# The first feed-forward's gates kept in the tile of the convolution's diagonals, its sums of rows a chunk later, and gate casts behind the PSUM copies

## The chip, the cores and the metric

The kernel runs on one core of one Trainium2 chip. Its engines are TensorE (PE, whose weight loads are shown apart as PEld), VectorE (DVE), ScalarE (ACT), GpSimd (POOL) and SyncE (SP), whose queue issues nearly all DMAs. The metric is the device time of one execution in microseconds. Before the change its median is 914.94 us over three runs (914.91 to 915.78).

## The reference

The reference is a small speech-encoder trunk over 256 tokens of width 1,024, in float32, with two layers. Each layer adds half a SwiGLU feed-forward, a token mixer, and another half feed-forward to the residual, each behind an RMS norm; the mixer is a convolution module in the first layer and latent attention in the second. A norm over the result ends it. What the change touches is the first feed-forward and, in one point, all four:

```python
def swiglu_ffn(h, w1, w3, w2):
    return (jax.nn.silu(h @ w1) * (h @ w3)) @ w2      # 1024 -> 2816 -> 1024

for i in range(DEPTH):
    h = h + FFN_RES_WEIGHT * swiglu_ffn(rmsnorm(h, ffn_norm1[i]), ffn1_w1[i], ffn1_w3[i], ffn1_w2[i])
    ...   # convolution module (i = 0, causal, depthwise, 31 taps) or attention (i = 1)
    h = h + FFN_RES_WEIGHT * swiglu_ffn(rmsnorm(h, ffn_norm2[i]), ffn2_w1[i], ffn2_w3[i], ffn2_w2[i])
return rmsnorm(h, final_norm)
```

## The kernel before, in words

**Products.** Every float32 operand is split into a rounded high part (`hi`, `Xh`, `Gh`) and the rest (`lo`, `Xl`, `Gl`). ACT writes the high part with a cast, DVE the low part with a subtraction (L246 and L247 for weights), and `mm3` (L330) makes one product from three matmuls: low by high, high by high, high by low.

**Weights.** They come in blocks of 128 x 2,048 float32, 1 MB each, in a list written at the start (`blocks`). A block lands in one of four `raw` buffers, is cast into one of five pairs of `hi` and `lo` buffers, and is then used by TensorE. `load_ahead` traces the load and the casts of the next blocks each time one is used. All loads stand in SP's one queue, in order, among the DMAs that turn the gates.

**A feed-forward** (`ffn_in`, L830) goes through the hidden width in chunks `c` = 0 to 5. Chunks 0 to 2 and 4 use four blocks each, 96 matmuls; chunk 5 is half as wide and uses two. A chunk ends with a SiLU on ACT (L948), a multiplication on DVE (L950), and `turn` (L835). `turn` brings the gates into the layout that the second half needs: a DVE transposition in blocks of 32 (L467, tile `gt`), four DMAs to DRAM (L471, `gd`) and one back (L476, tile `gb`), and then the casts into `Gh` (ACT, L841) and `Gl` (DVE, L842). The second half multiplies with `w2`, one block per 256 rows of it, in `Rows.block`.

**Seven products.** Chunk 3, and the first four blocks of `w2`, are computed with seven products of sums and differences instead of eight plain ones (`seven_products`, L366). Four weight blocks are loaded (`fetched`, L184), and DVE makes differences of whole blocks in place (L200, 128 x 2,048) beside the casts (L214, L200). On the other side stand four sums of rows of X, or of the gates of the first two chunks (`sums_of_rows`, L344), and their high and low parts (`forms_of`, L361 and L362). Between the products ACT copies two PSUM banks (L258 is the wrapper `urgent` through which such instructions are traced), and DVE adds the second copy, `kept`, to a bank (`c12`) before later products may write on.

**Where the rows for the sums come from.** For X, `whole_rows` (L347) adds the high and the low part into a `raw` buffer (L349), and the sums are made there in place. For the gates of the down products the second, third and fourth feed-forward let the turned gates of chunks 0 and 1 land in a tile of their own, `rows4` (`keep`), and sum there. In the first feed-forward (`X.whole`) `keep` is false: it adds `Gh` and `Gl` into a `raw` buffer as for X. There `rows4` holds other data: the convolution needs 64 diagonal blocks of 128 x 64 (`dpair`), the first 32 of which lie in `rows4`. The generator `diagonals` (L1659) has ACT write them (L1669), four at each call of `beside`, which the first feed-forward makes nine times in its chunks, four times behind the seven down products and then once for each block.

**What sets the order.** The order of the instructions on each engine is fixed when the kernel is built. A scheduler takes, of the instructions that its own clock has ready, the one traced first; `urgent` raises the priority, and `order(a, b)` demands that `a` comes behind `b`. On the chip each engine then follows its list and waits where an input is not there yet.

Of the kernel before, what the change touches and what calls it, by code (L numbers as in the profile page):

```python
# [11 lines left out]
F32 = mybir.dt.float32  # L12
# [10 lines left out]
NT = S // P  # L23
# [66 lines left out]
def trunk(ctx: ExitStack, tc: tile.TileContext, x, xt, first, pos, invf, gfin, wdw,  # L90
# [275 lines left out]
    def seven_products(xh, xl, forms, banks):  # L366


        def rows(a, tb):
            k = slice(4 * a, 4 * a + 4)  # L370
            return xh[:, k, tbs(tb)], xl[:, k, tbs(tb)]

        def product(a, b, fresh):
            load_ahead(W_BUFS - 1)
            (hi, lo), = weights(1, False)
            for k in range(4):
                c = slice(k * 512, k * 512 + 512)
                mm3(b, a[0][:, k], a[1][:, k], hi[:, c], lo[:, c], fresh and k == 0, k == 3, (), True)

        n0 = n_used[0]  # L380
        c11, c21, c12, c22 = banks[0, 0], banks[1, 0], banks[0, 1], banks[1, 1]
        product(rows(0, 0), c11, True)
        urgent(nc.scalar.copy)(c21, c11)
        product(forms[0], c22, True)
        kept = tmp.tile([P, 512], F32, tag="s", name=uid("p5"))
        urgent(nc.scalar.copy)(kept, c22)
        product(forms[1], c21, False)
        add = urgent(nc.vector.tensor_add)(c12, c21, kept)
        order(casts[n0 + 5, 0][1], add.ins)
        product(rows(1, 0), c11, False)  # L390
        product(forms[2], c21, False)
        add = urgent(nc.vector.tensor_add)(c22, c21, kept)
        order(casts[n0 + 6, 0][1], add.ins)
        product(forms[3], c12, False)
        product(rows(1, 1), c21, False)
# [8 lines left out]
    def tbs(tb):  # L404
        return slice(tb * P, (tb + 1) * P)
# [414 lines left out]


    n_ffns = [0]

    def ffn(X, make_next, beside=lambda: None, apart=False):
        n = n_ffns[0]
# [2 lines left out]
            return ffn_in(act, X, make_next, beside, apart, SEVEN_UP.get(n, ()), n in SEVEN_DOWN)  # L828

    def ffn_in(act, X, make_next, beside, apart, seven_up, seven_down):  # L830

        keep = seven_down and not X.whole
        Gh = act.tile([P, NF, S], F32R, tag="Gh", name=uid("Gh"))
        Gl = act.tile([P, NF, S], F32R, tag="Gl", name=uid("Gl"))
        def turn(c, tb, w, g):  # L835

            n = w // P
            f = slice(4 * c, 4 * c + n)
            bv = turn_blocks(act, g[:, :w], n, "g", (), rows4[:, 2 * c + tb, :] if keep and c < 2 else None)
            gh = Gh[:, f, tbs(tb)].rearrange("p t (i q) -> p t i q", q=32)  # L840
            nc.scalar.copy(gh, bv)  # L841
            nc.vector.tensor_sub(Gl[:, f, tbs(tb)].rearrange("p t (i q) -> p t i q", q=32), bv, gh.bitcast(F32))  # L842

        def first_chunk(X, u):

# [27 lines left out]
        for c in range(6):  # L873

            both = c == 5
            w = 256 if both else 512
            kn = HB // 512
            u = {}
            if c == 0 and X.pool:
                first_chunk(X, u)  # L880
            if seven_up and c == min(seven_up) - 2:
                forms = forms_of(sums_of_rows(*whole_rows(X.xh, X.xl)), Gh[:, 14:], Gl[:, 14:])
            if c in seven_up:
                for key in ((0, 0), (0, 1), (1, 1), (1, 0)):
                    u[key] = bank("A", "u")
                seven_products(X.xh, X.xl, forms, {(tb, m): b for (m, tb), b in u.items()})
                beside()
                beside()
            if both and seven_down:
                if keep:  # L890
                    z11, z21, z12, z22 = (rows4[:, n, :] for n in range(4))
                    down_sums = sums_of_rows(z11, z12, z21, z22)
                else:
                    down_sums = sums_of_rows(*whole_rows(Gh[:, :8], Gl[:, :8]))
                first_form = forms_of(down_sums[:1], *(act.tile([P, 2, S], F32R, tag=tag, name=uid(tag))
                                                       for tag in ("s1h", "s1l")))
            for m in range(0 if u else 1 if both else 2):
                parts = weights(KT // kn, c > 0 or m > 0)
                before = None
                if X.whole and c == 0 and m == 0:  # L900
                    load_to(4)
                for tb in range(NT):
                    u[m, tb] = bank("A", "u")
                steps = [(k, tb) for k in range(KT) for tb in range(NT)]
                if not (X.whole and c == 0 and m == 0):
                    steps.sort(key=lambda t: (t[0] // kn, t[1]))
                if not X.whole and c == 0 and m == 0:
                    steps.sort(key=lambda t: t[1])
                if X.whole and c == 0 and m == 0:

                    steps = [(k, tb, kind) for k in range(KT) for kind in "hlx" for tb in range(NT)]
                elif X.whole and c == 0:

                    steps = [*((k, tb, kind) for i in (0, 2) for kind in ("hx", "l") for tb in range(NT)
                               for k in (i, i + 1)), *((k, tb, "lhx") for k, tb in steps[2 * kn:])]
                for i, (k, tb, *kinds) in enumerate(steps):
                    hi, lo = parts[k // kn]
                    j = k % kn
                    after = X.between if X.between and c == 0 and m == 0 and i == 2 else ()
                    args = (X.xh[:, k, tbs(tb)], X.xl[:, k, tbs(tb)], hi[:, j * 512:(j + 1) * 512],  # L920
                            lo[:, j * 512:(j + 1) * 512])
                    if not X.whole and c == 0 and m == 0 and i == KT:

                        after = (first_mm,)
                    if kinds and m == 0:
                        some(u[m, tb], kinds[0], *args, (k, kinds) == (0, ["h"]), (k, kinds) == (KT - 1, ["x"]))
                    elif kinds:
                        mm = some(u[m, tb], kinds[0], *args, (k, kinds[0]) == (0, "hx"), k == KT - 1)
                        if before is not None:
                            order(mm, before.ins)  # L930
                        before = mm if k < kn else None
                    else:
                        first_mm = mm3(u[m, tb], *args, k == 0, k == KT - 1, after)
                    if X.whole and c == 0 and m == 0:
                        if i == 5:
                            for q in range(NT):
                                fetch(h[q], x[tbs(q), :])
                    if X.whole and c == 0 and m == 1 and i == KT + 2 * kn:
                        for q in range(NT):
                            X.rms(q)  # L940
                    if c == 0 and m == 0 and i == (KT - 1 if X.between is None else 1):
                        X.late()
                        load_ahead()
                if c > 0:
                    beside()
            for tb in range(NT):
                s = tmp.tile([P, 512], F32, tag="s", name=uid("s"))
                nc.scalar.activation(s[:, :w], u[0, tb][:, :w], AF.Silu, scale=X.r[tb])  # L948
                mul = urgent(nc.vector.tensor_mul) if c in seven_up or c + 1 in seven_up else nc.vector.tensor_mul
                mul(s[:, :w], s[:, :w], u[0, tb][:, w:] if both else u[1, tb])  # L950
                turn(c, tb, w, s)
        o = Rows(Gh, Gl, NF, make_next is Final, seven_down)
        if seven_down:
            both = (xp.tile([P, KT, S], F32R, tag=tag, name=uid("rows")) for tag in ("Xh", "Xl"))
            o.seven({**first_form, **forms_of(down_sums[1:], *both)})
            for _ in range(4):
                beside()
        for i in range(4 if seven_down else 0, NF // 2 - (3 if apart else 2)):
            o.block(i)
            beside()  # L960
        return o.finish(X.rh, make_next, act, apart)
# [697 lines left out]
    def diagonals():  # L1659
        fetch(dw, wdw)  # L1660
        fetch(wp2, wpair)

        ident2 = dpair[1][:, KP - 1, :]
        nc.gpsimd.tensor_tensor(ident2, ident[:, :64], ident[:, 64:], op=ALU.add)
        n = 4
        for g in range(2):
            for j in range(0, KP, n):
                for k in range(j, j + n):
                    nc.scalar.activation(dpair[g][:, k, :], ident2, AF.Copy, scale=wp2[:, g, k:k + 1])  # L1669
                yield  # L1670

    class Rows512:

# [5 lines left out]

    rows = Rows512()  # L1680

    todo = diagonals()

    def beside():
# [117 lines left out]
```

## Time and profile before

| | us |
|---|---|
| median of three runs | 914.94 |
| profiled execution | 911.86 |
| its span, first to last instruction | 910.0 |
| TensorE busy in the span | 889.0 |
| DVE busy | 769.2 |
| ACT busy | 581.1 |

The granted TensorE clock is 0.996 over the span. A row of a timeline begins with start and duration and ends with the idle time of that engine just before, and what ended it. A row of waits has the engine and line that waited, what for, the total, how often, and the longest. A matmul row lists longer than matmuls are apart, since they are pipelined.

The first feed-forward takes the first 195 us. Its chunks begin at about 5, 30, 52, 75 (the seven up products), 94 and 117 us, the seven down products at 127, and the remaining blocks of `w2` at 156.

### The profile page before, as it was taken

What the parts mean: (1) busy time and instruction counts of PE and PEld (TensorE: products, weight loads), DVE (VectorE), ACT (ScalarE), POOL (GpSimd) and SP (SyncE); (2) the same over time, 40 slices, a digit from 0 to 9 for tenths busy, and PEclk for the clock granted to TensorE, in tenths of its full rate; (3) what the DMA queues carried; (4) which work ended last, traced back from release to release, by engine and by line L of the source; (5) the groups of instructions that cost most, each with busy time, mean ns of one, the idle gap of its engine ahead of it and who ended that gap; (6) DMA issues with size and microseconds to landing.
All of it is one profiled execution on the core that took longest, in us unless ns stands there. A gap on an engine that the chain in (4) does not pass through costs nothing.

```text
span 910.0 us, 12272 instructions
## 1 busy us (share of the span) xinstructions
PE 889.0 (98%) x4209; PEld 742.7 (82%) x4209; DVE 769.2 (85%) x1105; ACT 581.1 (64%) x1005; POOL 107.0 (12%) x227
## 2 busy tenths in 40 slices
PE   9899997999999999999999999999999999999997
PEld 7788875899998888888888878878899888878886
DVE  6899998659998989999588989995768579989963
ACT  7896646569896555756476456673767576464752
POOL 1100000039982000000010000000500010000000
PEclk9999999999999999999999999999999999999999
DMA  9794946825414793958848459297544449278551
GB/s 334 284 315 128 332 122 255 343 93 211 161 47 105 282 352 93 349 171 307 318 141 332 162 191 361 75 377 239 189 176 171 154 141 350 93 266 299 162 215 47
DMA packets 71054, 198.94 MB, mean 219 GB/s; under 512 B 12368, under 2 KB 41936, under 8 KB 51664
## 3 DMA queue, kind: packets, MB, share of 16 engines
q1 hardware_dynamic: 70560, 197.47, 61.2%
q8 instruction: 33, 0.54, 0.2%
q10 hardware_dynamic: 432, 0.69, 0.2%
q14 instruction: 29, 0.24, 0.1%
HBM read 181.87 MB, written 16.25 MB: 218 GB/s over the span
## 4 chain that ended last, share of the span: by engine, by line
PE 72%; DVE 12%; DMA 9%; issue 3%; ACT 2%; SPq 1%; POOL 1%; DVEq 0%; ACTq 0%
PE u L332 10%; PE u L336 10%; PE u L335 10%; PE o L332 8%; PE o L336 8%; PE o L335 8%; DVE lo L200 4%; PE u L993 3%; PE gate L993 3%; PE o L1229 2%; DMA gd<-gt 2%; DVE raw L200 2%; DMA raw<-in_f1w 2%; DVE lo L247 1%; SPq L471 1%
## 5 line engine op out<-in xcount | busy, mean ns | idle before, releaser
L247 DVE TENSOR_TENSOR lo<-raw,hi 128x1024 fp32r<-128x1024 f32 (+1 forms) x228 | 266.9, 1211 | 33.0 <-ACT hi L246 31.3
L246 ACT CAST hi<-raw 128x1024 fp32r<-128x1024 f32 (+1 forms) x230 | 228.7, 1047 | 81.8 <-DMA raw<-in_f2w 26.3
L332 PE MATMUL u<-lo,Xh 128*128 128x512 f32 x592 | 231.2, 391 | 3.2 <-DVE lo L247 2.6
L335 PE MATMUL u<-hi,Xh 128*128 128x512 f32 x592 | 230.4, 389 | 0.0
L336 PE MATMUL u<-hi,Xl 128*128 128x512 f32 x592 | 230.1, 389 | 0.0
L214 ACT CAST hi<-raw 128x1024 fp32r<-128x1024 f32 x112 | 111.6, 1052 | 63.5 <-DVE raw L200 51.9
L200 DVE TENSOR_TENSOR lo<-raw,hi 128x1024 fp32r<-128x1024 f32 x112 | 132.3, 1215 | 11.3 <-ACT hi L214 11.2
L332 PEld LDWEIGHTS u<-lo,Xh 128*128 128x128 f32 x592 | 111.1, 188 | 28.5 <-DVE lo L247 4.0
L336 PEld LDWEIGHTS u<-hi,Xl 128*128 128x128 f32 x592 | 111.1, 188 | 23.5 <-DVE Xl L454 0.5
L335 PEld LDWEIGHTS u<-hi,Xh 128*128 128x128 f32 x592 | 111.1, 188 | 22.9
L332 PE MATMUL o<-lo,Gh 128*128 128x512 f32 (+1 forms) x276 | 107.1, 390 | 5.8 <-DVE lo L200 5.8
L335 PE MATMUL o<-hi,Gh 128*128 128x512 f32 (+1 forms) x276 | 107.1, 388 | 0.0
L336 PE MATMUL o<-hi,Gl 128*128 128x512 f32 (+1 forms) x276 | 107.0, 388 | 0.0
L426 POOL TENSOR_TENSOR ms<-ss 128x1 f32<-128x1 f32 x16 | 9.9, 622 | 608.9 <-ACT junk L418 608.9
L200 DVE TENSOR_TENSOR raw<-raw,raw 128x2048 f32<-128x2048 f32 x32 | 73.1, 2283 | 0.6 <-DMA raw<-in_f2w 0.3
L332 PEld LDWEIGHTS o<-lo,Gh 128*128 128x128 f32 x276 | 52.1, 189 | 18.1 <-DVE lo L200 7.8
L336 PEld LDWEIGHTS o<-hi,Gl 128*128 128x128 f32 x276 | 52.1, 189 | 10.7
L335 PEld LDWEIGHTS o<-hi,Gh 128*128 128x128 f32 x276 | 52.1, 189 | 10.4
L1082 DVE SCALAR_TENSOR_TENSOR acc<-V,dw,acc 128x128 f32<-128x128 f32 (+1 forms) x174 | 53.9, 395 | 0.1
L1103 ACT ACTIVATE prod<-V,dw 128x128 f32<-128x128 f32 (+1 forms) x128 | 45.9, 419 | 2.0 <-POOL Y L1104 1.0
L841 ACT CAST Gh<-gb 128x512 fp32r<-128x512 f32 (+1 forms) x36 | 20.6, 574 | 37.2 <-DMA gb<-gd 37.2
L786 DVE SCALAR_TENSOR_TENSOR h<-o,rh,h 128x512 f32<-128x512 f32 (+1 forms) x18 | 12.9, 719 | 29.4 <-PE o L336 29.4
(269 smaller groups left out, 1315.4 us busy)
## 6 DMA issues: line engine op xcount, KB each, us to landing
raw<-in_f2w SPq DMA_DIRECT2D x66, 1024.0 KB, 6.5
raw<-in_f1w SPq DMA_DIRECT2D x62, 1024.0 KB, 7.2
raw<-in_cw SPq DMA_DIRECT2D x12, 1024.0 KB, 5.8
gd<-gt SPq DMA_DIRECT2D x160, 64.0 KB, 2.9
gb<-gd SPq DMA_DIRECT2D x28, 256.0 KB, 2.9
raw<-in_wo SPq DMA_DIRECT2D x4, 1024.0 KB, 4.8
hd<-rows SPq DMA_DIRECT2D x56, 64.0 KB, 2.3
rows<-hd SPq DMA_DIRECT2D x14, 256.0 KB, 2.7
```

Of the source, the lines that this page charges most:

```text
L200: ins = nc.vector.tensor_sub(out, left, right)
L214: casts[n, i] = nc.scalar.copy(hi[:, c], raw[:, c]), sub(lo[:, c], raw[:, c], hi[:, c].bitcast(F32))
L246: casts[len(loaded), i] = (nc.scalar.copy(hi[:, c], raw[:, c]), low.tensor_sub(lo[:, c], raw[:, c], hi[:, c].bitcast(F32)))
L247: low.tensor_sub(lo[:, c], raw[:, c], hi[:, c].bitcast(F32)))
L332: mm = nc.tensor.matmul(o, ah, bl, start=start, stop=False, skip_group_check=seeded)
L335: nc.tensor.matmul(o, ah, bh, start=False, stop=False, skip_group_check=seeded)
L336: return nc.tensor.matmul(o, al, bh, start=False, stop=stop, skip_group_check=seeded)
L841: nc.scalar.copy(gh, bv)
L993: mm = nc.tensor.matmul(u[:, t], w[:, c], X.x[:, k, t], start=(k == 0), stop=(k == KT - 1))
L1082: dve_last.append(nc.vector.scalar_tensor_tensor(out if j == j1 - 1 else y, v, w, y, op0=ALU.mult, op1=ALU.add))
L1103: prods_last.append(nc.scalar.activation(p, v, AF.Copy, scale=w))
L1229: p = nc.tensor.matmul(o[tb, d], (Zl if kind == "x" else Zh)[:, f, tbs(tb)], (lo if kind == "l" else hi)[:, c], start=(f, kind) == (0, "l" ...
```

## The change

- In the first feed-forward too, the turned gates of chunks 0 and 1 land in `rows4`, and the sums for the down products are made there. The addition of `Gh` and `Gl` into a `raw` buffer falls away.
- The diagonals that lie in `rows4` are written later. The generator now writes 31 of the other group first; then it only yields until `stage` says "down", which is set behind the seven down products. Then it writes the 32 in `rows4`, and last the one that takes the place of the folded identity. The four calls of `beside` behind the down products become one more call before each block.
- In the first feed-forward the sums of X are traced at the start of chunk 2 instead of chunk 1.
- In every feed-forward the casts of the last two turned gates are ordered in the seven products: `Gh` on ACT behind the copy `kept`, `Gl` on DVE behind the first addition. In the up products these are the gates of chunk 2, in the down products those of chunk 5.

```diff
         kept = tmp.tile([P, 512], F32, tag="s", name=uid("p5"))
-        urgent(nc.scalar.copy)(kept, c22)
+        last = urgent(nc.scalar.copy)(kept, c22)
         product(forms[1], c21, False)
         add = urgent(nc.vector.tensor_add)(c12, c21, kept)
         order(casts[n0 + 5, 0][1], add.ins)
+        for high, low in gates[-NT:]:
+            order(high, last.ins)
+            order(low, add.ins)
...
     def ffn_in(act, X, make_next, beside, apart, seven_up, seven_down):
-        keep = seven_down and not X.whole
+        first_form = {}
...
-            bv = turn_blocks(act, g[:, :w], n, "g", (), rows4[:, 2 * c + tb, :] if keep and c < 2 else None)
+            bv = turn_blocks(act, g[:, :w], n, "g", (), rows4[:, 2 * c + tb, :] if seven_down and c < 2 else None)
             gh = Gh[:, f, tbs(tb)].rearrange("p t (i q) -> p t i q", q=32)
-            nc.scalar.copy(gh, bv)
-            nc.vector.tensor_sub(Gl[:, f, tbs(tb)].rearrange("p t (i q) -> p t i q", q=32), bv, gh.bitcast(F32))
+            low = Gl[:, f, tbs(tb)].rearrange("p t (i q) -> p t i q", q=32)
+            gates.append((nc.scalar.copy(gh, bv), nc.vector.tensor_sub(low, bv, gh.bitcast(F32))))
...
-            if seven_up and c == min(seven_up) - 2:
+            if seven_up and c == min(seven_up) - (1 if X.whole else 2):
                 forms = forms_of(sums_of_rows(*whole_rows(X.xh, X.xl)), Gh[:, 14:], Gl[:, 14:])
...
             if both and seven_down:
-                if keep:
-                    z11, z21, z12, z22 = (rows4[:, n, :] for n in range(4))
-                    down_sums = sums_of_rows(z11, z12, z21, z22)
-                else:
-                    down_sums = sums_of_rows(*whole_rows(Gh[:, :8], Gl[:, :8]))
+                z11, z21, z12, z22 = (rows4[:, n, :] for n in range(4))
+                down_sums = sums_of_rows(z11, z12, z21, z22)
...
             o.seven({**first_form, **forms_of(down_sums[1:], *both)})
-            for _ in range(4):
-                beside()
+        stage.append("down")
         for i in range(4 if seven_down else 0, NF // 2 - (3 if apart else 2)):
+            beside()
             o.block(i)
             beside()
...
-        n = 4
-        for g in range(2):
-            for j in range(0, KP, n):
-                for k in range(j, j + n):
-                    nc.scalar.activation(dpair[g][:, k, :], ident2, AF.Copy, scale=wp2[:, g, k:k + 1])
-                yield
+        for g in (1, 0):
+            for j in range(KP - g):
+                nc.scalar.activation(dpair[g][:, j, :], ident2, AF.Copy, scale=wp2[:, g, j:j + 1])
+                if j % 4 == 3:
+                    yield
+            if g == 1:
+
+                while "down" not in stage:
+                    yield
+        nc.scalar.activation(ident2, ident2, AF.Copy, scale=wp2[:, 1, KP - 1:])
```

More of the change, by code (lines that the diff above doesn't have):

```diff
@@ L822, in trunk @@
     n_ffns = [0]
+    gates = []
     def ffn(X, make_next, beside=lambda: None, apart=False):
@@ L1680, in trunk @@
     rows = Rows512()
+    stage = []
     todo = diagonals()
```

## The prediction

> **What bounds the kernel now.** I read the busy times first, then TensorE's waits, then TensorE's timeline at each of them.
>
> ```profile
> PE 889.0 (98%) x4209; PEld 742.7 (82%) x4209; DVE 769.2 (85%) x1105; ACT 581.1 (64%) x1005; POOL 107.0 (12%) x227
> ```
> ```profile
> PE o L332 <- DVE lo L200: 8.1, 5, 3.9
> PE u L332 <- DVE lo L247: 2.6, 1, 2.6
> PE u L332 <- DVE u L258: 2.3, 2, 1.6
> ```
> ```profile
> 30.42 0.50 PE L332 MATMUL u<-lo,Xh 128*128 128x512 f32 x1 [2.55 <-DVE lo L247]
> ...
> 134.60 0.50 PE L332 MATMUL o<-lo,rows 128*128 128x512 f32 x1 [2.04 <-DVE lo L200]
> ...
> 141.56 0.79 PE L332 MATMUL o<-lo,Gh 128*128 128x512 f32 x1 [3.86 <-DVE lo L200]
> ...
> 145.49 0.51 PE L332 MATMUL o<-lo,Gh 128*128 128x512 f32 x1 [1.01 <-DVE lo L200]
> ...
> 153.57 0.50 PE L332 MATMUL o<-lo,Gh 128*128 128x512 f32 x1 [0.98 <-DVE lo L200]
> ...
> 537.47 0.50 PE L332 MATMUL u<-lo,Gh 128*128 128x512 f32 x1 [0.77 <-DVE u L258]
> ...
> 805.20 0.50 PE L332 MATMUL u<-lo,Gh 128*128 128x512 f32 x1 [1.56 <-DVE u L258]
> ```
>
> TensorE is busy for 98% of the span, so all that can be won is its waits, and nearly all of them stand in the first feed-forward: 2.55 us where its second chunk begins, and 2.04 + 3.86 + 1.01 + 0.98 = 7.9 us in its seven down products. The other feed-forwards lose 0.77 and 1.56 us, each behind the add of L258 in the seven up products.
>
> Why the fourth down product is late stands in the chain of waits, and what VectorE (DVE) has to do around it in the stages' busy times:
>
> ```profile
> 132.81 0.61 DVE rows L362
> 133.43 5.69 DMA raw<-in_f1w
> ...
> 139.20 1.05 ACT hi L214
> ...
> 140.28 1.22 DVE lo L200
> ```
> ```profile
> 28.00:50.00 22.00, 19.45 (x84) 15.80 (x85) 20.91 (x40) 22.00 (x52) 0.00 (x0) 1.00 0.78 285
> 50.00:74.70 24.70, 24.70 (x110) 20.46 (x109) 23.29 (x23) 20.89 (x51) 0.00 (x0) 1.00 0.65 218
> 74.70:153.50 78.80, 70.52 (x300) 56.32 (x298) 73.88 (x78) 47.33 (x60) 0.00 (x0) 0.98 0.64 213
> 153.50:194.30 40.80, 40.73 (x184) 33.80 (x185) 25.90 (x26) 22.53 (x29) 0.95 (x3) 1.00 0.78 298
> ```
> ```profile
> 351.90:420.50 68.60, 68.60 (x304) 56.62 (x304) 65.82 (x69) 44.32 (x55) 0.00 (x0) 1.00 0.68 238
> ```
> ```profile
> 141.50:146.00 4.50, 3.43 (x8) 2.28 (x9) 4.50 (x5) 4.50 (x7) 0.00 (x0) 0.65 0.10 27
> ```
>
> (Columns: stretch, its length, busy time and instructions of PE, PEld, DVE, ACT, POOL, then clock, DMA share, GB/s.) The sums of rows of the down products lie in a "raw" buffer. Its last reader, the DVE subtraction of L362, ends at 133.42; 0.01 us later the weight load that needs the buffer goes out, takes 5.69 us, and the fourth product waits for it. The second feed-forward keeps its gates in rows4 and has no such load: there the same stretch, from chunk 2's gates to the last down cast, takes 68.6 us with TensorE busy all the time. In the first it takes 78.8 with DVE busy for 73.88: DVE is the chain, and it stood idle for 4.9 us. The row from 141.50 is what follows the 3.86 us wait: at a mean granted clock of 0.65 eight matmuls kept TensorE busy for 3.43 us, where 184 took 40.73 from 153.5 on, 0.22 each; the wait costs some 3.43 - 8 x 0.22 = 1.6 us more.
>
> **Part 1, gates kept in rows4 (the first feed-forward's down products).**
>
> ```profile
> 108.94 2.29 DVE L349 TENSOR_TENSOR xs<-Gh,Gl 128x2048 f32<-128x2048 f32 x1
> ...
> 140.28 1.22 DVE L200 TENSOR_TENSOR lo<-raw,hi 128x1024 fp32r<-128x1024 f32 x1 [3.67 <-ACT hi L214]
> ```
>
> One DVE addition of 2.29 us goes, since the turned gates already stand in float32; the four sums and their forms stay, in place. The raw buffer isn't taken, so the load of 133.43 can go when a cast frees a buffer, and the 3.67 us that DVE waited behind it go. The gate DMAs land in another tile, as many as before, and no queue gets more of them. On the DVE chain: 2.29 + 3.67 = 6.0 us. The other 1.2 us of DVE's idle time (casts that wait for gates to land) I leave. Bounds: 2.3, if something else keeps the load late, and 7.2, if all 4.9 us of idle time go. The slow matmuls add nothing: TensorE waited for DVE behind them too.
>
> **Part 2, the up sums one chunk later.**
>
> ```profile
> 21.02 2.29 DVE L349 TENSOR_TENSOR xs<-Xh,Xl 128x2048 f32<-128x2048 f32 x1
> 23.35 2.14 DVE L344 TENSOR_TENSOR xs<-xs 128x512 f32<-128x512 f32 x3
> 27.94 0.69 DVE L362 TENSOR_TENSOR Gl<-xs,Gh 128x512 fp32r<-128x512 f32 x1 [2.44 <-ACT Gh L361]
> ...
> 29.15 1.22 DVE L247 TENSOR_TENSOR lo<-raw,hi 128x1024 fp32r<-128x1024 f32 x1
> ...
> 74.71 0.69 DVE L258 TENSOR_TENSOR s<-s,u 128x512 f32<-128x512 f32 x1 [1.35 <-PE u L336]
> ```
> ```profile
> 21.39 1.98 POOL L426 TENSOR_TENSOR ms<-ss 128x1 f32<-128x1 f32 x1 [16.65 <-ACT junk L418]
> ...
> 25.55 0.19 POOL L426 TENSOR_TENSOR ms<-ss 128x1 f32<-128x1 f32 x1
> ```
> ```profile
> 26.71 0.69 ACT L948 ACTIVATE s<-u,R 128x512 f32<-128x512 f32 x1 [0.79 <-POOL R L429]
> 27.30 0.61 ACT L361 CAST Gh<-xs 128x512 fp32r<-128x512 f32 x1
> 27.80 1.99 ACT L246 CAST hi<-raw 128x1024 fp32r<-128x1024 f32 x2
> ```
> ```profile
> 20.00:22.50 2.50, 2.50 (x13) 2.07 (x12) 2.47 (x2) 2.50 (x8) 1.11 (x1) 1.00 1.02 415
> ```
>
> Chunk 1's first weights are cast at 27.80 because ACT's queue holds two SiLUs that wait for the row norms, and then a cast of the sums. The norms were slow: the same POOL addition took 1.98 us beside the DVE addition of 21.02 to 23.31, and 0.19 later. Without the sums there, the norms come some 1.8 us earlier, the 0.5 us of the sums' cast goes, and DVE's 0.6 at 28.55 with it: 2.9, so the whole wait of 2.55 can go, if the weights are there. At 415 GB/s a 1,024 KB load needs 2.5 us, so by my estimate they land soon after 22.5. Bounds: 0.5 (the cast alone) and 2.55.
>
> The Trainium skill, "SBUF — State Buffer", section "SBUF: two separate sides", says that a VectorE operation with two SBUF inputs and a GpSimd operation that reads SBUF lock each other out for a whole instruction; the 1.98 us ending 0.06 us after the addition agree. By that rule this term is 2.55; were the two unrelated, it would be 1.1.
>
> But the first 5.0 us of these sums (2.29 + 2.14 + 0.6) now fall into DVE's work between 29 and 74.7. Its casts there begin some 3.1 us earlier, and there are 1.35 us of idle time at 74.71 and 22.0 - 20.9 = 1.1 in the stage from 28 on to fill, beside the small operations of the rope tables:
>
> ```profile
> 37.29 0.16 DVE L1354 CAST pf<-pi 128x2 f32<-128x2 int32 x1
> ...
> 50.63 0.19 DVE L1379 TENSOR_SCALAR red_abs<-red_abs 128x64 f32<-128x64 f32 x1
> ```
>
> They are 22, from the one row to the other, of 0.16 to 0.23 us: about 4.2. They are due only in the attention layer, and the sums, traced earlier, push them out. If nothing is filled or pushed out, DVE comes to 74.7 later by 5.0 - 3.1 = 1.9 us; at most it comes 2.5 earlier, with TensorE, whose wait before that is 2.55. I take 1.0 earlier, between the ends and nearer to the upper one, as half of the rope work alone makes 2.1. The new sums also take a raw buffer in chunk 2; three other buffers turn over there, and the four loads of the up products come after it.
>
> **Part 3, gate casts behind the PSUM copies.**
>
> ```profile
> 532.54 0.62 ACT L841 CAST Gh<-gb 128x512 fp32r<-128x512 f32 x1 [1.42 <-DMA gb<-gd]
> 533.07 0.58 ACT L258 COPY p<-u 128x512 f32<-128x512 f32 x1
> ```
> ```profile
> 800.28 0.62 ACT L841 CAST Gh<-gb 128x512 fp32r<-128x512 f32 x1 [2.22 <-DMA gb<-gd]
> ```
>
> In the third and fourth feed-forward ACT waits 1.42 and 2.22 us for a turned gate to land, and the copy that the add of L258 needs stands behind it. The copy now goes first, during that wait. The gate's cast still stands before the next weight cast, if the order is otherwise kept, so that cast gains only the copy's 0.5 us: 2 x 0.5 = 1.0 us. Bounds: 0 and 0.77 + 1.56 = 2.3. The down products' last gates are needed only by the last blocks; their casts are hidden by all the blocks between, and cost 0.
>
> **Part 4, the diagonals.**
>
> ```profile
> L1669 ACT ACTIVATE rows<-dpair,wpair 128x64 f32<-128x64 f32 x32 | 8.1, 354 | 0.0
> ```
>
> There are still 64, but 32 move behind the down products: 8.1 us of ACT between 153.5 and 194.3, where it is busy 22.5 of 40.8 us. That idle time hides them: 0, and up to 8.1 if they stand in one piece ahead of a weight cast. They are first read in the convolution.
>
> **The sum.** The DVE chain to the last down product: 6.0 + 1.0 = 7.0 us; from there to 194.3 TensorE was busy 40.73 of 40.80 us, so it carries what it is given to the end. With part 3: 8.0. The profiled execution took 911.86 us (span 910.0 and 1.86 around it), 3.1 below the median of 914.94; it would be 903.9, and the median 906.9.
>
> **The rivals.**
> - *All waits go.* If the rope work leaves and DVE's idle time is filled, TensorE alone decides: 2.55 + 7.9 + 1.6 (slow matmuls) + 2.3 (part 3) = 14.3 us, 900.6. For it: the second feed-forward runs so. Against: DVE needs 73.88 - 2.29 = 71.6 us where TensorE needs 68.6.
> - *DVE is the bound everywhere, and only its removed work counts:* 2.3 + 1.0 = 3.3 us, 911.6. For it: the sums pushed into chunk 2 cost what the earlier start gives, and another late cast takes the place of the late load. Against: the 3.67 us of idle time have one cause, and it is taken away. The Trainium skill, "Perfetto Trace Analysis", section "Identifying the Most-Contended Engine", would have the engine of highest occupancy bound the kernel, with TensorE judged by weight loads: DVE's 85% against 82% here, which gives this case.
> - *Nothing is won:* the late load is moved to the up products, whose sums hold a raw buffer now, and the chain is as long as it was: 914.9.
> - *Slower:* the diagonals are set free just when the down products end, where TensorE has no lead (its 153.57 waited for DVE). If all 32 stand ahead of the next weight casts, TensorE waits 8.1 us and 1.6 for the slow matmuls: 9.7 - 8.0 = +1.7, 916.6. It decides from some 25 diagonals in a row, at 8.1 / 32 = 0.25 us each. For it: ACT's order is fixed at build time. Against: four are released at a time, between blocks.
>
> **How the numbers follow.** My forecast has 0.50, with its own range 904.0 to 909.5; all waits go 0.16; removed work alone 0.20; nothing 0.04; slower 0.10. A measurement of this kernel can tell about 0.2%, 1.8 us. Faster 0.86, same 0.04, slower 0.10. The range from 900 to 913 leaves out the last two cases and the lower edge of the second.
>
> **What would show it.** Right: no addition of L349 after the up sums, no wait over 2 us in the seven down products, the stretch of 78.8 us at 71 to 74, POOL's first addition well under 1 us, chunk 1 beginning within 1 us, the copy of L258 ahead of the gate casts, diagonals between 140 and 190. Wrong: a new wait for casts in the seven up products or in the first down blocks, a load that waits for L362 in chunk 2, or the wait behind the last products as long as before.

## The result, and the profile after

The changed kernel takes 905.83 us (904.73 to 906.04, four runs), beside 915.26 us for the kernel before in the same session: a ratio of 0.9894 (0.9877 to 0.9911), faster by 1.1%. The profiled execution took 905.75 us, with a span of 903.8. One execution in this document, 926.13 us of part 2 alone, counts as slow and is left out of the ratios. Line numbers have moved: L426, L429, L841 and L1669 of before are L429, L432, L845 and L1667 after.

Busy times and TensorE's waits of the changed kernel:

```profile
PE 890.2 (98%) x4209; PEld 744.1 (82%) x4209; DVE 765.3 (85%) x1104; ACT 580.7 (64%) x1005; POOL 104.2 (12%) x227
```
```profile
PE u L332 <- DVE lo L200: 4.8, 2, 2.9
...
PE o L332 <- DVE lo L200: 0.4, 2, 0.3
```

The waits of the down products, 8.1 us before, are down to 0.4, and the wait of 2.6 for a cast of L247 is gone. In their place stand 4.8 us in the first feed-forward's seven up products (`u`), where TensorE waited 0.47 before. TensorE's timeline shows where each kernel stands at the same matmul, first after, then before (with 30.42 and 153.57 of the prediction; 153.57 and 148.87 are the first matmul of the seventh down product):

```profile
27.33 0.39 PE L332 MATMUL u<-lo,Xh 128*128 128x512 f32 x1
...
73.57 0.39 PE L332 MATMUL u<-lo,Gh 128*128 128x512 f32 x1
...
79.33 0.80 PE L332 MATMUL u<-lo,Gh 128*128 128x512 f32 x1 [2.88 <-DVE lo L200]
...
94.82 0.50 PE L332 MATMUL u<-lo,Xh 128*128 128x512 f32 x1 [1.88 <-DVE lo L200]
...
131.97 0.39 PE L332 MATMUL o<-lo,Gh 128*128 128x512 f32 x1
...
148.87 0.50 PE L332 MATMUL o<-lo,Gh 128*128 128x512 f32 x1 [0.17 <-DVE lo L200]
```
```profile
77.23 0.39 PE L332 MATMUL u<-lo,Gh 128*128 128x512 f32 x1
...
91.46 0.50 PE L332 MATMUL u<-lo,Xh 128*128 128x512 f32 x1 [0.47 <-DVE lo L200]
...
126.95 0.39 PE L332 MATMUL o<-lo,Gh 128*128 128x512 f32 x1
```

| the same matmul | before | after | after is ahead by |
|---|---|---|---|
| chunk 1 begins | 30.42 | 27.33 | 3.1 |
| first sum of rows in the up products | 77.23 | 73.57 | 3.7 |
| the seventh up product begins (rows of X again) | 91.46 | 94.82 | -3.4 |
| down products begin | 126.95 | 131.97 | -5.0 |
| the seventh down product begins | 153.57 | 148.87 | 4.7 |
| end of the span | 910.0 | 903.8 | 6.2 |

So 3.7 us are won before the up products, 8.7 are lost from there to the down products, 9.7 are won in these up to the seventh, and 1.5 later. The change moved the waits forward more than it took them away, and made them smaller.

The stages' busy times show why, the changed kernel first, from DVE's first weight cast of chunk 1 to its last cast of the down products:

```profile
25.70:148.80 123.10, 117.81 (x500) 95.31 (x499) 118.03 (x141) 87.09 (x157) 0.00 (x0) 0.97 0.67 232
72.40:148.80 76.40, 71.11 (x294) 56.64 (x293) 72.05 (x76) 53.83 (x90) 0.00 (x0) 0.96 0.61 212
79.30:82.20 2.90, 2.87 (x7) 2.29 (x8) 2.90 (x4) 2.90 (x4) 0.00 (x0) 0.50 0.31 93
94.80:98.30 3.50, 3.48 (x10) 2.77 (x11) 3.50 (x4) 3.08 (x8) 0.00 (x0) 0.66 0.91 323
```
```profile
29.10:153.50 124.40, 114.66 (x492) 92.58 (x492) 116.97 (x139) 89.12 (x159) 0.00 (x0) 0.99 0.67 228
```

DVE is busy for 118.03 of 123.1 us after, and was for 116.97 of 124.4 before. It starts 3.4 us earlier and stands idle for 5.1 us where it stood for 7.4 (2.4 less), but has 1.1 us more to do, since the sums of X now lie inside the stretch: 3.4 + 2.4 - 1.1 = 4.7, as in the table. The last two rows of after are the price of the new waits beside the waits themselves: behind each, TensorE ran for some 3 us at a mean granted clock of 0.50 and 0.66.

### The profile page after: what moved, and what is told of

Read it like the earlier page. It is cut to its first block, busy times and chain, and to the rows that moved or that the text cites. A ratio compares the mean times of both kernels' runs of the same rounds, so it can differ in the third digit from the quotient of the medians.

```text
span 903.8 us, 12258 instructions
## 1 busy us (share of the span) xinstructions
PE 890.2 (98%) x4209; PEld 744.1 (82%) x4209; DVE 765.3 (85%) x1104; ACT 580.7 (64%) x1005; POOL 104.2 (12%) x227
## 4 chain that ended last, share of the span: by engine, by line
PE 76%; DVE 11%; DMA 6%; issue 2%; ACT 2%; SPq 1%; DVEq 0%; ACTq 0%
PE u L332 11%; PE u L336 11%; PE u L335 11%; PE o L332 8%; PE o L335 8%; PE o L336 8%; DVE lo L200 3%; PE u L993 3%; PE gate L993 3%; DMA raw<-in_f2w 3%; DVE raw L200 2%; PE u L403 2%; PE o L1229 2%; DVE lo L247 1%; DMA hd<-rows 1%
## 5 line engine op out<-in xcount | busy, mean ns | idle before, releaser
L247 DVE TENSOR_TENSOR lo<-raw,hi 128x1024 fp32r<-128x1024 f32 (+1 forms) x228 | 266.8, 1211 | 35.0 <-ACT hi L246 33.7
L429 POOL TENSOR_TENSOR ms<-ss 128x1 f32<-128x1 f32 x16 | 8.1, 512 | 607.2 <-ACT junk L421 607.2
L845 ACT CAST Gh<-gb 128x512 fp32r<-128x512 f32 (+1 forms) x32 | 18.0, 565 | 32.2 <-DMA gb<-gd 32.2
```

Source lines behind the costliest of these rows:

```text
L247: low.tensor_sub(lo[:, c], raw[:, c], hi[:, c].bitcast(F32)))
```

## The experiments

Every kernel computes the whole reference. A ratio is to the runs of the kernel before on the same chip, with its 95% interval.

### Each part alone, and the kernel before again

Parts 1 and 4 alone (the gates in `rows4` and the diagonals), against the changed kernel:

```diff
-        for high, low in gates[-NT:]:
-            order(high, last.ins)
-            order(low, add.ins)
...
-            if seven_up and c == min(seven_up) - (1 if X.whole else 2):
+            if seven_up and c == min(seven_up) - 2:
```

> Parts 1 and 4 alone: the gates in rows4 and the diagonals later; the up sums stay in chunk 1 and the gate casts are not ordered. My theory (the DVE chain to the last down product is given 2.29 us of work and 3.67 us of waiting): 6.0 us faster, some 909.3, with the 2.55 us wait at chunk 1 as before and no wait over 2 us in the seven down products. Rival, that only the removed work counts: 2.3 us, 913.0. Rival, that the later sums carry the gain: no difference.

Part 2 alone, against the kernel before:

```diff
-            if seven_up and c == min(seven_up) - 2:
+            if seven_up and c == min(seven_up) - (1 if X.whole else 2):
```

> Part 2 alone: the up sums traced in chunk 2, all else as before. My theory: the wait at chunk 1 goes (2.55 us), but DVE does the sums later and the late load of the down products stays, so that the chain gives most of it back: 1.0 us faster, 914.3. Rival, that each wait counts by itself: 2.5 us, 912.8. Rival, that the sums of the up products now hold the raw buffer at the wrong time: slower by some 3 us or more.

Part 3 alone, against the kernel before:

```diff
-        urgent(nc.scalar.copy)(kept, c22)
+        last = urgent(nc.scalar.copy)(kept, c22)
...
+        for high, low in gates[-NT:]:
+            order(high, last.ins)
+            order(low, add.ins)
```

> Part 3 alone: the casts of the last two gates behind the PSUM copy and the first addition, in all four feed-forwards. Forecast: 1.0 us, 914.3, with half of the waits of 0.77 and 1.56 us left in the third and fourth feed-forward. Rival, since the changed kernel shows both waits gone: 2.3 us, 913.0. Rival, that those waits went by another part: no difference.

The kernel before, unchanged, as a fourth kernel of the same session:

> The kernel before, once more with a profile. Its profiled execution took 911.86 us, and its other runs 914.9 to 915.8. If the profiled one was lucky, this profile shows some 914 to 916 and a wait that the first didn't have, of about 3 us; if the difference is in what lies around the span, the span is again 910.

| kernel | median us (range), ten runs each | ratio |
|---|---|---|
| before again | 912.56 (909.38 to 920.22) | 1.0003 (0.9976 to 1.003) |
| parts 1 and 4 | 908.87 (906.94 to 912.02) | 0.9942 (0.9921 to 0.9963) |
| part 2 | 917.24 (912.35 to 926.13) | 1.003 (1.001 to 1.005) |
| part 3 | 910.33 (909.27 to 913.65) | 0.9963 (0.9947 to 0.9978) |

By the ratios, and with 913.8 us for the kernel before on this chip (31 runs), part 1 alone gives 5.3 us (interval 3.4 to 7.2), part 3 gives 3.4 (2.0 to 4.8), and part 2 alone *costs* 2.7 (0.9 to 4.6). The kernel before again has neither the 914 to 916 us nor the span of 910 that were expected of its profile, but 909.38 us and a span of 907.5. Its waits differ from those of the first profile, 0.51, 3.58 and 2.29 us in the down products where the prediction shows 2.04, 3.86, 1.01 and 0.98. TensorE's timeline of part 2 alone, then of part 1 alone:

```profile
79.55 0.50 PE L332 MATMUL u<-lo,Gh 128*128 128x512 f32 x1 [2.88 <-DVE lo L200]
...
143.77 0.79 PE L332 MATMUL o<-lo,Gh 128*128 128x512 f32 x1 [4.19 <-DVE lo L200]
```
```profile
30.79 0.50 PE L332 MATMUL u<-lo,Xh 128*128 128x512 f32 x1 [2.83 <-DVE lo L247]
...
94.67 0.50 PE L332 MATMUL u<-lo,Xh 128*128 128x512 f32 x1 [2.27 <-DVE lo L200]
...
582.06 0.69 PE L332 MATMUL o<-lo,rows 128*128 128x512 f32 x1 [2.19 <-ACT o L258]
```

Part 2 alone takes the start wait away (no wait at chunk 1), brings the same 2.88 us as the changed kernel in the up products, and leaves the late load with its 4.19. That this makes up the 2.7 us isn't shown: its profile also has waits of 1.16 us (372.49) and 2.17 us (810.19) in feed-forwards that the edit doesn't touch. Part 1 alone takes the late load away and has no wait over 0.5 us in the first feed-forward's down products, but brings 2.27 late in the up products. So the 2.88 belongs to part 2, and the wait near 95 comes with part 1: it is 0.47 us before and 0.90 with part 2 alone.

The wait at 582.06 is new to the reading: in another feed-forward's *down* products a PSUM copy came late. ACT's timeline of part 1 alone shows what stood before it:

```profile
574.31 0.62 ACT L842 CAST Gh<-gb 128x512 fp32r<-128x512 f32 x1 [7.48 <-DMA gb<-gd]
...
580.92 0.61 ACT L842 CAST Gh<-gb 128x512 fp32r<-128x512 f32 x1
581.43 0.58 ACT L258 COPY o<-o 128x512 f32<-128x512 f32 x1
```

ACT waited for a gate to land and then ran without a pause to the copy, with one more gate cast directly ahead of it. Both gates are 512 wide and so belong to chunk 4; part 3 orders those of chunk 5 alone.

### Each part taken out of the changed kernel

Part 2 undone, with the last two lines of the first diff above:

> The changed kernel with part 2 undone: the up sums in chunk 1 again. The forecast's part 2 was worth 1.0 us, so 906.8. Rival, from the profiles of the changed kernel and of parts 1 and 4 alone (the later sums cost the up products more than chunk 1 won): 904.5. Rival, that chunk 1's wait counts by itself: 908.4.

The addition kept, into `rows4` instead of a `raw` buffer, so that its 2.29 us come back and the late load does not:

```diff
-            ... rows4[:, 2 * c + tb, :] if seven_down and c < 2 else None)
+            ... rows4[:, 2 * c + tb, :] if seven_down and not X.whole and c < 2 else None)
...
+                if X.whole:
+                    y = rows4.rearrange("p n c -> p (n c)").rearrange("p (k t) -> p k t", t=S)
+                    nc.vector.tensor_add(y, Gh[:, :8].bitcast(F32), Gl[:, :8].bitcast(F32))
+                    down_sums = sums_of_rows(*(y[:, 4 * a:4 * a + 4, tbs(tb)] for tb in range(2) for a in range(2)))
...
```

> The changed kernel with the addition of the high and low gates back in the first feed-forward, but into rows4 and not into a raw buffer, so that it tells the 2.29 us of work from the buffer. My theory (DVE is the chain up to the last down product): 2.3 us slower than the changed kernel, 908.1. Rival, that only the late load counted: 905.8. It also takes the down sums out of the up products, since they must wait for the addition; if those matter more, it is faster than 905.8.

The order of part 3 taken out (the three lines of the loop), and the changed kernel once more:

> The changed kernel with part 3 undone. By the forecast's price of part 3: 1.0 us slower than the changed kernel, 906.8. By the run of part 3 alone (3.4 us, since the gates often land later than in the one profile and hold up the PSUM copies of the down products too): 909, with runs that spread over several us where the changed kernel's lie within 1.3.

> The changed kernel once more, beside the others on one chip: 905.8, with the waits of 2.9 and 1.9 us in the up products again, if they are fixed by the order of the instructions and not by chance.

| kernel | median us (range), runs | ratio |
|---|---|---|
| changed, again | 906.01 (904.35 to 906.72), 5 | 0.9915 (0.9901 to 0.9929) |
| without part 2 | 906.4 (904.81 to 907.46), 4 | 0.992 (0.9901 to 0.9938) |
| addition kept | 908.7 (908.49 to 909.64), 4 | 0.9948 (0.9933 to 0.9964) |
| without part 3 | 908.79 (907.64 to 910.02), 6 | 0.9947 (0.9935 to 0.996) |

Within the changed kernel part 2 is worth nothing that can be measured (906.4 and 906.01, intervals on top of each other). Part 3 is worth 908.79 - 906.01 = 2.8 us, about what it gave alone; without it the runs do not spread more (2.4 us in both kernels), as they were expected to. The addition costs 908.7 - 906.01 = 2.7 us, its 2.29 and a little more, although TensorE had no wait left in the down products that could have shown it. TensorE's timeline of that kernel tells where it came out, followed by the one without part 2:

```profile
79.50 0.50 PE L332 MATMUL u<-lo,Gh 128*128 128x512 f32 x1 [2.88 <-DVE lo L200]
...
89.33 0.50 PE L332 MATMUL u<-lo,Gh 128*128 128x512 f32 x1 [2.47 <-DVE u L258]
```
```profile
30.23 0.80 PE L332 MATMUL u<-lo,Xh 128*128 128x512 f32 x1 [2.42 <-DVE lo L247]
...
94.79 0.66 PE L332 MATMUL u<-lo,Xh 128*128 128x512 f32 x1 [2.27 <-DVE lo L200]
```

With the addition back, a wait of 2.47 us stands in the *up* products, where the changed kernel has 0.36. DVE's timeline has the addition there, ahead of the add of L258 that TensorE waits for; that add stands at 88.59, and at 86.08 in the changed kernel:

```profile
75.38 2.28 DVE L895 TENSOR_TENSOR rows<-Gh,Gl 128x2048 f32<-128x2048 f32 x1
...
88.59 0.69 DVE L258 TENSOR_TENSOR u<-u,p 128x512 f32<-128x512 f32 x1
```

Without part 2 the same total is paid as 2.42 at the start instead of 2.88 in the up products. One chain on DVE, and a wait wherever TensorE meets it, fits both (the 2.88 has a second cause on ACT, below). Without part 3, ACT's timeline shows the order that the forecast described, in the fourth feed-forward, with TensorE behind it (1.11 us at 801.25):

```profile
796.33 0.62 ACT L842 CAST Gh<-gb 128x512 fp32r<-128x512 f32 x1 [1.77 <-DMA gb<-gd]
796.85 0.58 ACT L258 COPY p<-u 128x512 f32<-128x512 f32 x1
```

The changed kernel again has the waits of 2.88 us (79.85) and 1.87 us (95.34), as expected, and one more, in the second down product, that its first profile does not have:

```profile
135.63 0.50 PE L332 MATMUL o<-lo,s1h 128*128 128x512 f32 x1 [1.76 <-DVE s L950]
```

DVE is 1.1 us later there than in the first profile. Most of it arises at one difference of weight blocks, which DVE starts at 120.27 after waiting 2.07 us for a weight load, and at 119.12 after 1.14 us in the first profile.

### Can the new waits be ordered away?

The four sums of the down products run on DVE inside the changed kernel's up products (L344 from 75.21 on, below). In the next kernel they come behind the last addition of these:

```diff
-    def sums_of_rows(x11, x12, x21, x22):
+    def sums_of_rows(x11, x12, x21, x22, after=None):
...
-            nc.vector.tensor_tensor(out, left, right, op=op)
+            ins = nc.vector.tensor_tensor(out, left, right, op=op)
+            if after is not None:
+                order(ins, after.ins)
...
+        added[0] = add
...
-                down_sums = sums_of_rows(z11, z12, z21, z22)
+                down_sums = sums_of_rows(z11, z12, z21, z22, added[0] if X.whole else None)
```

> The changed kernel, with the first feed-forward's four down sums ordered on DVE behind the last addition of the up products (the schedule had put them between the casts of the up products). If those sums make the waits of 2.88 and 1.88 us there, 2.5 us of DVE work and some of the slow clock go: 902.5 or less. Rival, that the later up sums alone make these waits: 905.8, as the changed kernel.

The same edit, with part 2 undone:

> The up sums in chunk 1 and the down sums behind the up products. If both crowd DVE in the up products, these wait 0.5 us, as before the change, the wait at chunk 1 is 2.5 us, and the time is some 902. Rival, that DVE's work only comes back later, in the down products: 905.

The sums of X at chunk 1, but their addition behind the casts of chunk 1's first three weight blocks, so that neither the norms nor those casts stand behind it:

```diff
-        nc.vector.tensor_add(x, xh.bitcast(F32), xl.bitcast(F32))
+        whole = nc.vector.tensor_add(x, xh.bitcast(F32), xl.bitcast(F32))
+        if n_ffns[0] == 1:
+            order(whole, casts[6, 1][1].ins)
...
-            if seven_up and c == min(seven_up) - (1 if X.whole else 2):
+            if seven_up and c == min(seven_up) - 2:
```

> The changed kernel with the up sums traced in chunk 1 again, but with their first addition ordered behind the casts of chunk 1's first three weight blocks. If chunk 1's wait comes from the sums standing ahead of those casts and beside POOL's norms, and the 2.9 us wait in the up products from sums that hold a raw buffer until 61 us, both go: 905.8 - 2.9 - 1.7 for the slow clock, 901.2. Rival, that DVE has too much work before the up products wherever the sums stand: a wait of some 3 us somewhere before 95 us, and 905.

And that with the down sums behind the up products:

> The run before this, with the down sums also ordered behind the up products. If the down sums take DVE time that the up products need: 1 to 2 us faster than without, 900. Rival, from the run that had only this order: the sums then come too late for the down products, and it is 1 us or more slower.

| kernel | median us (range), runs | ratio |
|---|---|---|
| down sums behind the up products | 909.99 (905.89 to 912.47), 10 | 0.996 (0.9936 to 0.9985) |
| the same, part 2 undone | 905.35 (903.74 to 908.69), 4 | 0.9918 (0.9889 to 0.9948) |
| sums of X behind the first casts | 906.1 (905.04 to 907.31), 5 | 0.9919 (0.9905 to 0.9932) |
| that, and the down sums later | 906.47 (905.06 to 912.48), 7 | 0.9924 (0.991 to 0.9939) |

None is told from the changed kernel on the better side. With part 2 undone and the down sums later, TensorE has no wait over 1 us in the up products: what was 2.27 near 95 with the sums early is 0.70 + 0.41 with them late (and 0.69 and 1.00 in the down products). So these four sums, early, make most of that wait; where the sums of X stand in chunk 2, though, moving them leaves 1.57 of 1.88 (at 94.24). And the total moves by no more than the runs scatter (905.35 and 906.4). With the sums of X behind the first casts the 2.88 is gone, and so is the wait at chunk 1, but two others stand in their place, and the kernel is no faster:

```profile
84.92 0.50 PE L332 MATMUL u<-lo,Gh 128*128 128x512 f32 x1 [1.97 <-DVE u L258]
...
94.06 0.79 PE L332 MATMUL u<-lo,Xh 128*128 128x512 f32 x1 [2.41 <-DVE lo L200]
```

With the down sums later alone, time is lost. TensorE's and ACT's timelines of that kernel in the down products:

```profile
138.64 0.79 PE L332 MATMUL o<-lo,rows 128*128 128x512 f32 x1 [3.16 <-ACT o L258]
```
```profile
136.09 2.02 ACT L1671 ACTIVATE rows<-dpair,wpair 128x64 f32<-128x64 f32 x8
138.01 0.58 ACT L258 COPY o<-o 128x512 f32<-128x512 f32 x1
```

Here eight diagonals stand in a row, 2.02 us, directly ahead of the PSUM copy that TensorE waits 3.16 us for. The kernel of the last line of the table has the same 3.16 with eight diagonals (2.01 us) ahead of the copy. The same edit with part 2 undone (905.35) has none ahead of that copy, and its wait there is 0.69 us:

```profile
133.60 0.50 PE L332 MATMUL o<-lo,rows 128*128 128x512 f32 x1 [0.69 <-ACT o L258]
```

So the diagonals make up most of the 3.16. They don't explain the whole loss, since the kernel of the last line has the same wait and a median of 906.47; why only the first of the two is slower stays open.

## Why the prediction was right, and where it was not

**Total: near, and partly by luck.** 906.9 was forecast and 905.83 measured. The forecast started from 914.94, the median of three runs; the kernel before had 913.8, 913.29 and 913.92 in later sessions (31, 13 and 11 runs), and against the last of these the changed kernel again gains 913.92 - 906.01 = 7.9 us, where the sum says 8.0. But the terms are not those of the sum: 5.3 instead of 6.0 for part 1 (alone), about 0 instead of 1.0 for part 2 and 2.8 instead of 1.0 for part 3 (both within the changed kernel). Errors of opposite sign cancel. From profile to profile the gain is 911.86 - 905.75 = 6.1 us; one execution of the kernel before can lie anywhere from 909.38 to 920.22, so that a pair of profiles can't decide between 6 and 9.

**Part 1: right, with one reading wrong.** 6.0 us forecast; 5.3 alone. The late load is gone with the buffer it waited for, and in the first profile none of the seven down products waits over 0.2 us (in the repeated one the second waits 1.76, above). The 2.29 is confirmed by putting it back (2.7). The 3.67 us of idle time were only partly a gain: DVE's idle time fell by 2.4 in the changed kernel. And "the four sums and their forms stay, in place" was wrong: before, the sums ran on DVE from 114 to 127 us, behind the addition and its buffer; from `rows4` they can run as soon as the gates have landed, and do so from 75.21 on (below), in the up products. There the wait near 95 comes with them, 1.9 to 2.4 us in every kernel with these sums early. They are the same DVE work in either place, and part 1 kept most of its gain.

**Part 2: the step that failed.** The start went as forecast. POOL's timeline of the changed kernel:

```profile
21.20 0.20 POOL L429 TENSOR_TENSOR ms<-ss 128x1 f32<-128x1 f32 x1 [16.63 <-ACT junk L421]
```

The addition took 0.20 us, 1.98 before, with no DVE addition beside it, and chunk 1 begins without a wait; ACT casts its weights as soon as they land, at 24.66, 3.1 us earlier, and DVE's first cast follows at 25.74, 3.4 earlier (the forecast has 2.9 in one place and 3.1 in another). This pair agrees with the rule of the Trainium skill, "SBUF — State Buffer", section "SBUF: two separate sides", by which the two engines lock each other out. What failed is "I take 1.0 earlier, between the ends": the 5 us of sums pushed into chunk 2 were to fill idle time and push the rope tables out. DVE's and SP's timelines of the changed kernel, and the row of before that answers to 73.01:

```profile
32.71 0.13 DVE L1354 CAST pf<-pi 128x2 f32<-128x2 int32 x1
...
40.22 2.29 DVE L349 TENSOR_TENSOR xs<-Xh,Xl 128x2048 f32<-128x2048 f32 x1
...
54.51 0.19 DVE L1379 TENSOR_SCALAR red_abs<-red_abs 128x64 f32<-128x64 f32 x1
...
61.02 0.68 DVE L362 TENSOR_TENSOR Gl<-xs,Gh 128x512 fp32r<-128x512 f32 x1
...
73.01 2.27 DVE L200 TENSOR_TENSOR raw<-raw,raw 128x2048 f32<-128x2048 f32 x1
75.21 0.68 DVE L344 TENSOR_TENSOR rows<-rows 128x512 f32<-128x512 f32 x1
...
78.05 1.22 DVE L200 TENSOR_TENSOR lo<-raw,hi 128x1024 fp32r<-128x1024 f32 x1 [0.97 <-ACT hi L214]
```
```profile
61.92 0.43 SPq L184 DMA_DIRECT2D raw<-in_f1w  x1
```
```profile
70.47 2.28 DVE L200 TENSOR_TENSOR raw<-raw,raw 128x2048 f32<-128x2048 f32 x1
```

The rope tables were not pushed out: they run from 32.71 to 54.51, and from 37.29 to 50.63 before. The sums held their `raw` buffer until 61.02 + 0.68 = 61.70, and the last of the four loads of the up products went out at 61.92. The difference of weight blocks that ran at 70.47 before runs at 73.01, behind chunk 2's gates. ACT could then not cast it at once:

```profile
76.49 0.59 ACT L258 COPY p<-u 128x512 f32<-128x512 f32 x1 [2.09 <-PE u L336]
76.97 7.68 ACT L214 CAST hi<-raw 128x1024 fp32r<-128x1024 f32 x8
```

The cast of 76.97 stands behind a PSUM copy that waits for TensorE until 76.49, though the difference was ready at 73.01 + 2.27 = 75.28; its low part follows at 78.05, and TensorE resumes at 79.33. That is the 2.88 us, at the same place and of the same size in all six profiles that hold part 2 with the sums of X in chunk 2.

It has the same size in all six because it is a round trip that TensorE starts itself. Its last matmul before the wait (76.06, 0.39 long) ends at 76.45; ACT copies that bank, then casts, DVE subtracts, and TensorE goes on at 79.33, 2.88 us later, however early DVE had the difference ready. Part of the wait is therefore the order on ACT and not work on DVE. In the last kernel of the last experiment table (profiled at 912.48 us, its slowest run) the difference is ready at 74.94, the casts stand ahead of that copy, and TensorE waits 1.35 us (77.91). That leaves some 1.2 to 1.5 us of the 2.88 to ACT's order; no run changes that order alone.

The forecast named this as a sign of being wrong ("a new wait for casts in the seven up products") and gave it no price. In the measure of the whole, part 2 is -2.7 us alone and about 0 in the changed kernel, where 1.0 was forecast.

**Part 3: right in kind, mis-sized.** 1.0 forecast with bounds of 0 and 2.3; 2.8 and 3.4 measured. The copy goes first now, as ACT's timeline of the changed kernel shows, and the two up-product waits of 0.77 and 1.56 no longer appear:

```profile
528.77 0.59 ACT L258 COPY p<-u 128x512 f32<-128x512 f32 x1 [0.18 <-PE u L336]
529.29 0.62 ACT L845 CAST Gh<-gb 128x512 fp32r<-128x512 f32 x1
```

But the copy was not what held the addition. DVE's timelines in the fourth feed-forward, without part 3 and then of the changed kernel:

```profile
799.36 1.22 DVE L200 TENSOR_TENSOR lo<-raw,hi 128x1024 fp32r<-128x1024 f32 x1 [1.69 <-ACT hi L214]
800.50 0.69 DVE L258 TENSOR_TENSOR u<-u,p 128x512 f32<-128x512 f32 x1
```
```profile
796.49 0.70 DVE L258 TENSOR_TENSOR u<-u,p 128x512 f32<-128x512 f32 x1 [1.53 <-PE u L336]
```

Without part 3 the copy ends at 796.85 + 0.58 = 797.43, and the addition starts 3.1 us later, behind the low part of a weight that waits for ACT's cast. In the changed kernel the addition stands ahead of that low part and waits for TensorE's product alone. The step that mis-sized the term is "so that cast gains only the copy's 0.5 us": the addition no longer waits for that cast, so the whole wait goes and not 0.5 of it. No run orders the copy without the gate's low part. In five profiles without the order the wait in the fourth feed-forward is 1.56, 1.24, 2.17, 1.07 and 1.11 us and that in the third 0 to 0.77, some 1.6 in all on average, where the forecast had one execution to price from. The rest of the 2.8 stays open. The wait of 2.19 at 582.06 is no part of it: it hangs on gates that part 3 doesn't order, and a kernel that holds part 3 (the last of the last experiment table) waits 2.08 us behind the same copy of the second feed-forward, at 409.32. Nor is a narrower spread of the runs: it was 10.8 us in ten runs of the kernel before and 4.4 with part 3 alone, but also 5.1 with part 1 alone.

**Part 4: right at 0, its time wrong.** The diagonals of `rows4` in the changed kernel:

```profile
L1667 ACT ACTIVATE rows<-dpair,wpair x32: 334/338/358, 94.0 to 146.3; 128x64 f32<-128x64 f32 x32
```

They begin at 94.0 and not after 140: each can go as soon as the sums have read its part of `rows4`. Up to twelve stand in a row, and no wait of TensorE over 0.2 us follows. The slower rival's mechanism is real, though: eight of them ahead of a PSUM copy cost most of a wait of 3.16 us in the kernel with late down sums, where the forecast had put the point at some 25. In the kernel that also has part 2 undone, 24 stand in a row (5.86 us from 138.05) ahead of a weight cast at 143.81, and TensorE waits 1.00 us for that weight at 146.16.

**Other signs and the rivals.** The stretch of 78.8 us was to become 71 to 74 and is 76.4 (72.40 to 148.80 above): the new waits lie in it, at a mean clock of 0.96. "All waits go" did not come, since waits of 4.8 us appeared; "only removed work counts" (911.6) is excluded by both medians. The Trainium skill, "Perfetto Trace Analysis", section "Identifying the Most-Contended Engine", led to that rival; the run differs from it, as part 3 removes no work and about half of part 1's gain came from removed waits. But the rival's core holds in a smaller place: between 25 and 149 us DVE is busy for 118 of 123 us, and that fits the addition's full price and that no move of sums gained what could be measured, not even the one without the 2.88. The price of slow matmuls in the rivals "all waits go" and "slower", 3.43 - 8 x 0.22, is 1.7 and not 1.6, which changes nothing.

## What to carry to other kernels

When an engine is busy for 95% of a stage, take work away from it there; moving its work to another place of the same stage only moves the wait, and the matmul where it surfaces may be far from the edit. On an in-order engine, look at what stands directly behind an instruction that waits for a DMA or for another engine, and let what is ready go first. Price such a wait from several executions: one wait here lay between 1.07 and 2.17 us in five, a difference as large as the forecast term. A wait that has the same size in every profile, like the 2.88, can be a chain that the waiting engine starts itself; look for it in the order of the other engines' lists.

## What the runs showed of the hardware

**A short wait of TensorE can cost more than its length.** Each of the six waits of 2.88 us was followed by a mean granted clock of 0.66 to 0.70 over 5 us, but not from the same moment: the first matmul behind it took 0.80 us in the changed kernel and 0.50 with part 2 alone. Rows of the kernels with part 2 alone and with the addition kept:

```profile
80.00:85.00 5.00, 5.00 (x17) 3.95 (x16) 5.00 (x5) 5.00 (x7) 0.00 (x0) 0.66 0.40 115
```
```profile
90.00:95.00 5.00, 5.00 (x17) 3.95 (x16) 5.00 (x5) 1.88 (x6) 0.00 (x0) 0.66 0.51 172
```

At 0.66 over 5 us TensorE loses 1.7 us, so that a wait of 2.88 sets it back by 4.6. Other waits can go either way: the wait of 1.88 at 94.82 was followed by a mean clock of 0.66, the same wait of 1.87 in the repeated run by 1.00, and so were those of 2.55 and 2.83 at chunk 1 (before, part 1 alone) and one of 3.58 (139.64, before again). What TensorE loses isn't always lost to the kernel: in the repeated run, where the clock stayed at 1.00 behind the 1.87, TensorE waited 1.76 us for DVE instead, at 135.63. The Trainium skill, "TensorE: Matmul & The Clock Gate", section "Part 1: The HAM clock gate (the "warmup" mystery)", has the clock decided in windows that run freely, without regard to the kernel; the varying start agrees with it.

**Equal kernels, unequal runs.** Ten runs of the kernel before span 10.8 us on one chip, with the same order of instructions in each. Among the waits that differ from profile to profile are those behind turned gates (1.07 to 2.17 us, above) and one behind a weight load (2.07 and 1.14 us in two profiles of the changed kernel).
